# Block fill, row transfers and weight loads in a two-layer trunk on one TensorE-bound core

## The chip, the cores and the metric

The kernel runs on one core of a Trainium2 chip. The metric is the device time of one execution in microseconds (us). Before the change the median of 3 runs is 988.75 us (987.04 to 989.66). Each trace shown is one execution taken by the profiler; line numbers such as L1272 are lines of the kernel before. The engines are PE (TensorE matmul; PEld its weight loads), DVE (VectorE), ACT (ScalarE), POOL (GpSimd) and SP, which here only issues DMAs.

## The reference

Sixteen learned meta tokens are put ahead of 512 tokens of width 1024; two layers follow, and a final RMSNorm. Each layer is `h + branch(rmsnorm(h))`. Layer 0 is gated linear attention with 4 heads (key width 256, value width 512), a decay from a rank-16 gate, and a SiLU gate:

```python
proj = xn @ w_in                               # q, k, v, z, g_lr
lg = log_sigmoid(g_lr @ w_gate_up + b_gate) / 16
# per head, causal:  o_i = sum_{j<=i} (q_i * exp(b_i - b_j)) . k_j  v_j,   b = cumsum(lg)
o = head_rms(o) * gnorm
y = (silu(z) * o) @ w_out
```

Layer 1 is differential softmax attention with 8 heads and a relative-position bias. All is float32.

## The kernel before

**Numbers.** Each float32 operand is split into a high part and a rest (`split`: ACT copies the high part, L270, DVE subtracts, L271), and three matmul passes stand for one product. The input projections use a Strassen-like scheme: a `Unit` handles 256 output columns as seven products of 12 matmuls of 264 columns (`product`, L403). In order they are, for a unit between two others: the one on `s21[0]` (bank bx), on `a12` (by), on `s21[1]` (bv), on `s43[1]` (bx again), the next unit's `a11` (bx), `a22` (by), `s43[0]` (bv). A bank that is written again must first have been read by ACT (`partial`, L424) or DVE (L449, L451, L453).

**Weights.** `load_blocks` (L282 to L288) brings 256 columns of a weight matrix, all 1024 rows, into one of two `raw` buffers, by two DMAs on SP of 512 KB each. The tile is [128, 4, 512]: block 2i+j holds column half i and row half j, and each DMA brings one column half, in pieces of 128 floats. `want_unit` makes from a raw tile, in this order: `a11` (block 0), sums of blocks 2, 3 and 0 (L338), the pair `s21` from the sums, `a12` (block 1), a further sum into block 1 and the pair `s43`, `a22` (block 3). When all of a tile's parts have been written into the program, the next load is, and on the chip it waits for the tile's last reader. `want_plain` takes the two column halves whole; it serves four loads at the start (8 of the 90 DMAs).

**Order of the work.** PE's order is that in which the program is written. `Weaver` holds a queue of background generators (units, output projections). `W.fill(us)` writes background matmuls into the program until their planned time is used up; a step of a unit is three matmuls and counts 0.33, of an output projection six and 0.68. `W.follow((us, fn))` calls a function after so much planned time; a function put on the list `behind` is called right after the next weight load is written, so that its DMA stands behind that load on SP. The order of the other engines is set by a scheduler that goes by priority and readiness.

**The blocks of a head.** `gla_blocks` (L1196 to L1292) goes over 5 token blocks: block 0 has the 16 meta tokens, blocks 1 to 4 have 128 each. `output(b)` does the matmuls (L1208 for block 0; L372 and L1214 otherwise) and the norm: ACT square with sum (L1217), DVE (L513), POOL power (L514), ACT scaled copy (L1219). `rows(b)` transposes the result on PE (L1272), gates it on DVE (L1274) and splits it. Its `fill` pairs are (0.6, 1.2) in heads 1 and 2 (`far`), (1.2, 1.2) in head 3 (`last`) and (1.9, 1.6) in head 0.

```python
for b in range(5):
    W.fill(fill[0] if b else 0.6)
    if prev is not None and (b == 1 or not far):
        rows(b - 1, prev)
    prev = output(b)
    ...
    W.fill(fill[1])
```

**Far rows.** In heads 1 and 2 only block 0 goes through `rows`; blocks 1 and 2, and 3 and 4, are turned by DMA (`far_rows`, L1222). Per block, ACT separates the 16-bit halves (L1233) and issues a write to DRAM (L1234), the pieces. After the second block `W.follow` waits 4.0 us of planned time and puts `turn` on `behind` (L1237). `turn` issues one transposing DMA on SP (L1240) into a part of `b_all` (called keep in the profile), and 11.0 us of planned time later `scaled_rows` gates (L1247) and splits what landed. The output projection that reads the rows is run in the next head; `W.land` forces all that is still open ahead of it.

Of the kernel before, what the change touches and what calls it, by code (L numbers as in the profile page):

```python
# [11 lines left out]
F32 = mybir.dt.float32  # L12
# [8 lines left out]
P = 128  # L21
# [52 lines left out]
class Weaver:  # L74
# [6 lines left out]
    def add(self, gen, us=0.0):  # L81
        self.queue.append(gen)
        self.left += us
        return gen
# [125 lines left out]
def trunk(ctx, tc, x, meta, g_norm, gla_w_in, gla_w_gate_up, gla_b_gate, gla_gnorm, gla_w_out,  # L210
# [3 lines left out]
    act, dve, pe, pool, sp = nc.scalar, nc.vector, nc.tensor, nc.gpsimd, nc.sync  # L214
# [8 lines left out]
    wp = ctx.enter_context(tc.tile_pool(name="wp", bufs=2))  # L223
# [8 lines left out]
    def T(p, shape, dt, tag, **kw):  # L232
        uid[0] += 1
        return p.tile(shape, dt, tag=tag, name=f"{tag}_{uid[0]}", **kw)
# [29 lines left out]
    def split(hi, lo, src, scale=None, keep=False):  # L264

        if keep:
            act.activation(hi, src, AF.Copy)
            kept.append(lambda: dve.tensor_tensor(lo, src, hi.bitcast(F32), op=ALU.subtract))
        elif scale is None:
            act.activation(hi, src, AF.Copy)  # L270
            dve.tensor_tensor(lo, src, hi.bitcast(F32), op=ALU.subtract)  # L271
        else:
            act.activation(hi, src, AF.Copy, scale=scale)
            dve.scalar_tensor_tensor(lo, src, scale, hi.bitcast(F32), op0=ALU.mult, op1=ALU.subtract)
# [4 lines left out]
        sp.dma_start(t, w[r0:r0 + nk * P, c0:c0 + ncol].rearrange("(k p) c -> p k c", p=P))  # L279
        return t  # L280

    def load_blocks(w, c0):  # L282

        t = T(wp, [P, 4, 512], F32, "raw")
        for i in range(2):
            sp.dma_start(t[:, 2 * i:2 * i + 2, :].rearrange("p j (k c) -> p (j k) c", k=4),
                         w[:, c0 + i * P:c0 + (i + 1) * P].rearrange("(k p) c -> p k c", p=P))
        return t  # L288

    W = Weaver()  # L290
    behind = W.behind
# [30 lines left out]

    def block_pair(src, keep=False):
        wh, wl = w_pair([P, 2, 512])
        split(wh, wl, src, keep=keep)
        return [[t[:, i, :] for t in (wh, wl)] for i in range(2)]

    def want_unit(w, c0, calm=False):
        def single(tag, b):
            def fn(raw):  # L330
                t = [T(wp, [P, 512], F32R, tag + part, bufs=1) for part in "hl"]
                with tc.issue_after(W.moved.ins) if calm and b == 0 else ExitStack():
                    split(*t, raw[:, b, :])
                return t
            return Part(tag, fn)

        def add(o, a, b):
            dve.tensor_tensor(o, a, b, op=ALU.add)  # L338

        def sums(raw):  # L340
            t = T(wp, [P, 2, 512], F32, "sum", bufs=1)
            add(t[:, 1, :], raw[:, 2, :], raw[:, 3, :])
            add(t[:, 0, :], t[:, 1, :], raw[:, 0, :])
            add(raw[:, 2, :], raw[:, 2, :], raw[:, 0, :])
            return t

        def outer(raw):
            add(raw[:, 1, :], raw[:, 1, :], su.t[:, 0, :])
            ws.room["sum"] += 1
            return block_pair(raw[:, 1:3, :])  # L350

        a11, a12, a22 = single("a11", 0), single("a12", 1), single("a22", 3)
        su = Part("sum", sums)
        s21 = Part("pair", lambda raw: block_pair(su.t))
        s43 = Part("pair", outer)
        ws.want((w, c0), [a11, su, s21, a12, s43, a22])
        return a11, a12, a22, s21, s43

    def want_plain(w, c0, keep=False):

        def first(raw):
            with behind_gate():
                return block_pair(raw[:, :2, :], keep)

        return ws.want((w, c0), [Part("pair", first),
                                 Part("pair", lambda raw: block_pair(raw[:, 2:, :]))])

    def mm3(ps, a, b, first=True, last=True, **kw):

# [826 lines left out]
    def gla_blocks(hd, s, fill, last, far):  # L1196

        s.y = None

        def val(b):  # L1200
            return [t[:, b - 1, :] for t in s.v]

        @urgent
        def output(b):
            t0, n = BLK[b]
            po = ps_tile()
            if b == 0:
                pe.matmul(po[:NM], s.am, s.vm, start=True, stop=True)  # L1208
            else:
                mm3(po, [t[:, t0 - NM:t0 - NM + P] for t in s.a], val(b), True, False)  # L1210
                for j in range(1, b):
                    c0 = ((b - 1) * (b - 2) // 2 + j - 1) * P
                    mm3(po, [t[:, c0:c0 + P] for t in s.c], val(j), False, False)
                pe.matmul(po, s.cm[:, (b - 1) * P:b * P], s.vm, start=False, stop=True)  # L1214
            on = tmp()[:, :512]
            st = T(tp, [P, 2], F32, "st")
            act.activation(on[:n], po[:n], AF.Square, accum_out=st[:n, 0:1])  # L1217
            rstd_of(st[:n, 1:2], st[:n, 0:1], G_HV, n)
            act.activation(on[:n], po[:n], AF.Copy, scale=st[:n, 1:2])  # L1219
            return on  # L1220

        def far_rows(pair):  # L1222

            yd = T(dp, [2, P, 2, 512], U16, "yd", bufs=2)
            src = yd.rearrange("m p h c -> (m p h) c")
            i = pair[0] - 1
            raw = b_all[:, i:i + 2, :].rearrange("p m c -> p (m c)")[:, :8 * P].rearrange("p (m c) -> p m c", m=4)
            left = [0, 1]

            @urgent  # L1230
            def leave(j, on):
                pl = words(tmp()[:, :512]).rearrange("p (h c) -> p h c", h=2)
                act.activation(pl, words(on).rearrange("p (c h) -> p h c", h=2), AF.Copy)  # L1233
                act.dma_start(yd[j], pl)  # L1234
                left.remove(j)
                if not left:
                    W.follow((4.0, lambda: behind.append((turn, s))), tag=s)  # L1237

            def turn():
                tc.keep_in_program_order(sp.dma_start(words(raw), src, transpose=True))  # L1240
                W.follow((11.0, lambda: scaled_rows(0)), (1.5, lambda: scaled_rows(1)), tag=s)

            def scaled_rows(j):
                t0, n = BLK[pair[j]]
                y = raw[:, :, j * P:(j + 1) * P]
                with tc.issue_after(W.mark.ins):
                    dve.tensor_tensor(y, y, s.z[:, :, t0:t0 + n], op=ALU.mult)  # L1247
                    for m0, m1, hi, lo in s.groups:
                        split(hi[:, :, t0:t0 + n], lo[:, :, t0:t0 + n], y[:, m0:m1, :])

            return leave

        def take_y():

            if not last:
                y = [T(gp, [P, 4, L], F32R, f"y{i}") for i in range(2)]
                return [[t[:, m, :] for m in range(4)] for t in y], [(0, 4, y[0], y[1])]

            qk = [T(gp, [P, 2, L], F32R, tag) for tag in ("qs", "ks")]
            hi = [qk[m // 2][:, m % 2:m % 2 + 1, :] for m in range(4)]  # L1260
            lo = [T(gp, [P, 1, L], F32R, "kd"), T(tp, [P, 1, L], F32R, "t"),
                  T(gp, [P, 1, L], F32R, "vm0"), T(wp, [P, 1, L], F32R, "sum", bufs=1)]
            return [[t[:, 0, :] for t in hi], [t[:, 0, :] for t in lo]], [(m, m + 1, hi[m], lo[m]) for m in range(4)]

        @urgent
        def rows(b, on):
            t0, n = BLK[b]
            if b == 0:
                s.y, s.groups = take_y()
            pt = ps_tile()  # L1270
            for m in range(4):
                pe.transpose(pt[:, m * n:(m + 1) * n], on[:n, m * P:(m + 1) * P], ident[:n, :n])  # L1272
            y = tmp()[:, :512].rearrange("p (m c) -> p m c", m=4)
            dve.tensor_tensor(y[:, :, :n], pt[:, :4 * n].rearrange("p (m c) -> p m c", m=4),  # L1274
                              s.z[:, :, t0:t0 + n], op=ALU.mult)
            for m0, m1, hi, lo in s.groups:
                split(hi[:, :, t0:t0 + n], lo[:, :, t0:t0 + n], y[:, m0:m1, :n])

        prev, leave = None, None
        for b in range(5):  # L1280
            W.fill(fill[0] if b else 0.6)
            if prev is not None and (b == 1 or not far):
                rows(b - 1, prev)
            prev = output(b)
            if far and b:
                if b % 2:
                    leave = far_rows((b, b + 1))
                leave(1 - b % 2, prev)
            W.fill(fill[1])
        if not far:  # L1290
            W.fill(2.0)
            rows(4, prev)  # L1292
# [18 lines left out]
    for hd in range(G_HEADS):  # L1311
        s = heads[hd]
# [610 lines left out]
```

## Time and profile before

| what | value |
|---|---|
| median of 3 runs | 988.75 us (987.04 to 989.66) |
| the profiled execution | 990.28 us, span 988.24 us |
| mean granted clock of TensorE | 0.995 |
| block loads, 512 KB each | 48 of `gla_w_in`, 42 of `diff_w_in` |
| their issue to landing, median | 4.5 and 5.5 us |
| transposes of far rows (L1240) | 4, on SP |
| DMA packets | 159945, of them 145277 under 2 KB |

The page gives busy time per engine over the span. The view of waits lists who stood idle for whom, with total, number and longest. The timeline shows each merged group with start and duration, and in brackets the idle time before it and what ended it. The view of windows gives, for stretches of the span, the length, each engine's busy time with its number of instructions (PE, PEld, DVE, ACT, POOL), the granted clock as a share of full speed, the DMA share and the GB/s. A duration on PE is that of a pipeline: the distance from one start to the next tells what an instruction costs.

### The profile page before, as it was taken

How to read it: one execution, taken by the hardware profiler on the slowest of the kernel's cores; microseconds unless marked ns; L12 is line 12 of the kernel's file. 1: busy time of each engine (PE TensorE's matmuls, PEld its weight loads, DVE VectorE, ACT ScalarE, POOL GpSimd, SP SyncE). 2: the span in 40 equal slices, each digit the busy share in tenths (PEclk: the TensorE clock that was granted, in tenths of full speed). 3: DMA queues.
4: the chain of work that ended last, by engine and by line, in shares of the span. 5: the costliest groups of instructions: out<-in, count | busy, mean ns of one | idle time of the engine just before them, and what ended most of it. 6: DMA issues, size and time to landing. Idle time of an engine off the chain costs nothing. (4 is left out here: it accounts for less than half of the span.)

```text
span 988.2 us, 18164 instructions
## 1 busy us (share of the span) xinstructions
PE 967.4 (98%) x7033; PEld 913.5 (92%) x7033; DVE 776.7 (79%) x1584; ACT 626.6 (63%) x1314; POOL 50.3 (5%) x68
## 2 busy tenths in 40 slices
PE   8999999999999999999999999999999999999997
PEld 8999999989999899999999998898998999988896
DVE  7889985876878599556998885977967879677785
ACT  7776755577636767536657675566764667654583
POOL 1000000000000100000000001001010000000001
PEclk9999999999999999999999999999999999999999
DMA  7332224634473353222332614235253352622212
GB/s 193 87 84 78 58 87 135 134 87 107 129 162 87 94 120 98 75 86 86 97 86 77 153 61 137 80 96 135 87 145 86 97 135 58 174 73 66 86 65 85
DMA packets 159945, 100.45 MB, mean 102 GB/s; under 512 B 41565, under 2 KB 145277, under 8 KB 159856
## 3 DMA queue, kind: packets, MB, share of 16 engines
q1 hardware_dynamic: 155824, 91.71, 34.7%
q10 hardware_dynamic: 4032, 7.55, 2.1%
q8 instruction: 56, 0.92, 0.4%
q14 instruction: 33, 0.27, 0.1%
HBM read 83.64 MB, written 9.67 MB: 94 GB/s over the span
## 5 line engine op out<-in xcount | busy, mean ns | idle before, releaser
L271 DVE TENSOR_TENSOR wl<-raw,wh 128x1024 fp32r<-128x1024 f32 x98 | 119.6, 1222 | 24.6 <-ACT wh L270 17.4
L270 ACT ACTIVATE wh<-raw 128x1024 fp32r<-128x1024 f32 x98 | 103.0, 1054 | 53.3 <-PE by L940 19.1
L403 PE MATMUL bv<-x,wh 128*128 128x264 f32 (+1 forms) x656 | 99.5, 290 | 0.2
L403 PE MATMUL bx<-x,wh 128*128 128x264 f32 (+1 forms) x640 | 95.2, 286 | 1.1 <-ACT wh L270 1.0
L403 PEld LDWEIGHTS bv<-x,wh 128*128 128x128 f32 x656 | 88.2, 192 | 1.3 <-DVE t L449 0.4
L403 PEld LDWEIGHTS bx<-x,wh 128*128 128x128 f32 x640 | 84.9, 189 | 2.4 <-ACT wh L270 1.6
L393 PE MATMUL bx<-x,wh 128*128 128x512 f32 (+1 forms) x256 | 62.5, 386 | 0.0
L271 DVE TENSOR_TENSOR wl<-sum,wh 128x1024 fp32r<-128x1024 f32 x41 | 50.1, 1222 | 14.4 <-ACT wh L270 13.0
L424 ACT ACTIVATE u<-bx 128x264 f32<-128x264 f32 (+1 forms) x120 | 45.3, 379 | 18.5 <-PE bx L403 17.0
L1657 ACT ACTIVATE p<-p,st 128x528 f32<-128x528 f32 (+3 forms) x64 | 36.4, 569 | 32.0 <-DVE st L1655 31.6
L403 PE MATMUL bv<-x,wl 128*128 128x264 f32 (+1 forms) x328 | 55.6, 286 | 0.1
L1693 POOL TENSOR_TENSOR st<-st,mhalf 128x1 f32<-128x1 f32 x32 | 31.1, 973 | 467.4 <-ACT on L1691 389.1
L270 ACT ACTIVATE wh<-sum 128x1024 fp32r<-128x1024 f32 x41 | 43.3, 1056 | 17.1 <-DVE sum L338 9.6
L403 PE MATMUL bx<-x,wl 128*128 128x264 f32 (+1 forms) x320 | 53.9, 285 | 0.0
L393 PEld LDWEIGHTS bx<-x,wh 128*128 128x128 f32 x256 | 44.5, 188 | 8.0
L270 ACT ACTIVATE a11h<-raw 128x512 fp32r<-128x512 f32 x41 | 25.8, 628 | 36.5 <-DMA raw<-in_diff_w_in_dram 18.1
L403 PE MATMUL by<-x,a12h 128*128 128x264 f32 (+1 forms) x320 | 46.7, 286 | 0.5 <-DVE tick L584 0.5
L403 PE MATMUL bx<-x,a11h 128*128 128x264 f32 (+1 forms) x320 | 46.2, 285 | 0.6 <-DVE hT L948 0.6
L403 PEld LDWEIGHTS bv<-x,wl 128*128 128x128 f32 x328 | 46.3, 190 | 0.4 <-issue 0.3
L403 PEld LDWEIGHTS bx<-x,wl 128*128 128x128 f32 x320 | 45.0, 188 | 0.8 <-DVE wl L271 0.5
L403 PEld LDWEIGHTS bx<-x,a11h 128*128 128x128 f32 x320 | 42.0, 188 | 1.4 <-DVE hT L948 0.8
L403 PEld LDWEIGHTS by<-x,a12h 128*128 128x128 f32 x320 | 41.7, 188 | 0.9 <-DVE tick L584 0.9
(483 smaller groups left out, 2640.3 us busy)
## 6 DMA issues: line engine op xcount, KB each, us to landing
raw<-in_gla_w_in_dram SPq DMA_DIRECT2D x48, 512.0 KB, 4.5
raw<-in_diff_w_in_dram SPq DMA_DIRECT2D x42, 512.0 KB, 5.5
raw<-in_diff_w_in_dram SPq DMA_DIRECT2D x11, 1024.0 KB
raw<-in_gla_w_out_dram SPq DMA_DIRECT2D x8, 1024.0 KB, 5.0
raw<-in_diff_w_out_dram SPq DMA_DIRECT2D x8, 1024.0 KB
vd<-planes ACTq DMA_DIRECT2D x12, 268.0 KB, 3.2
vd<-keep ACTq DMA_DIRECT2D x8, 264.0 KB, 2.3
T<-bdr SPq DMA_DIRECT2D x8, 264.0 KB, 5.2
```

The source lines that it names most:

```text
L270: act.activation(hi, src, AF.Copy)
L271: dve.tensor_tensor(lo, src, hi.bitcast(F32), op=ALU.subtract)
L393: pe.matmul(bank, a[:, k, :], b[k] if n0 is None else b[k][:, n0 + i * nn:n0 + (i + 1) * nn], start=n == 0 and ks[0] == 0, stop=n == len(t ...
L403: pe.matmul(bank[:, :x[q].shape[2]], w[p][:, k * P:(k + 1) * P], x[q][:, k, :], start=first and i == 0, stop=i == len(PASSES) - 1, skip_gr ...
L424: W.moved = act.activation(t, self.bx[:, :self.n], AF.Copy, scale=self.sc)
L1657: act.activation(p[:, :nk], p[:, :nk], AF.Exp, scale=-1.0, bias=st[:, m:m + 1], accum_out=st[:, 2 + m:3 + m])
L1693: pool.tensor_tensor(ms, ms, mhalf[:, :1], op=ALU.pow)
```

## The change

Three things are changed. In `gla_blocks`, the fill around block 0 becomes 1.6 behind its output and 1.9 ahead of its rows, in all heads (head 0 had these values). In `far_rows`, `turn` is called itself after the 4.0 us of planned time instead of being put behind the next weight load. `load_blocks` makes its tile [128, 8, 256] and brings a row half in each DMA, in pieces of 256 floats; a block is then a strided view of it (`block`), and the further sum goes into block 0 instead of block 1. The loads of `want_plain` stay by columns (`by_cols`).

```diff
-    def load_blocks(w, c0):
-        t = T(wp, [P, 4, 512], F32, "raw")
-        for i in range(2):
-            sp.dma_start(t[:, 2 * i:2 * i + 2, :].rearrange("p j (k c) -> p (j k) c", k=4),
-                         w[:, c0 + i * P:c0 + (i + 1) * P].rearrange("(k p) c -> p k c", p=P))
+    def load_blocks(w, c0, by_cols=False):
+        t = T(wp, [P, 8, 2 * P], F32, "raw")
...
+        for j in range(2):
+            sp.dma_start(t[:, 4 * j:4 * j + 4, :],
+                         w[512 * j:512 * j + 512, c0:c0 + 2 * P].rearrange("(k p) c -> p k c", p=P))
         return t
+    def block(raw, b):
+        i, j = divmod(b, 2)
+        return raw[:, 4 * j:4 * j + 4, i * P:(i + 1) * P]
...
-            add(t[:, 1, :], raw[:, 2, :], raw[:, 3, :])
+            add(in_rows(t[:, 1, :]), block(raw, 2), block(raw, 3))
...
-            add(raw[:, 1, :], raw[:, 1, :], su.t[:, 0, :])
+            add(block(raw, 0), block(raw, 1), in_rows(su.t[:, 0, :]))
             ws.room["sum"] += 1
-            return block_pair(raw[:, 1:3, :])
+            return block_pair(raw[:, :4, :])
...
                 if not left:
-                    W.follow((4.0, lambda: behind.append((turn, s))), tag=s)
+                    W.follow((4.0, turn), tag=s)
...
-            W.fill(fill[0] if b else 0.6)
+            W.fill(0.6 if b == 0 else 1.9 if b == 1 else fill[0])
...
-            W.fill(fill[1])
+            W.fill(fill[1] if b else 1.6)
```

More of the change, by code (lines that the diff above doesn't have):

```diff
@@ L280, in load_w, with in_rows @@
         return t
-    def load_blocks(w, c0):
-        t = T(wp, [P, 4, 512], F32, "raw")
-        for i in range(2):
-            sp.dma_start(t[:, 2 * i:2 * i + 2, :].rearrange("p j (k c) -> p (j k) c", k=4),
-                         w[:, c0 + i * P:c0 + (i + 1) * P].rearrange("(k p) c -> p k c", p=P))
-        return t
+    def load_blocks(w, c0, by_cols=False):
+        t = T(wp, [P, 8, 2 * P], F32, "raw")
+        if by_cols:
+            t = t.rearrange("p k (i c) -> p (k i) c", c=P)
+            for i in range(2):
+                sp.dma_start(t[:, 8 * i:8 * i + 8, :],
+                             w[:, c0 + i * P:c0 + (i + 1) * P].rearrange("(k p) c -> p k c", p=P))
+            return t
+        for j in range(2):
+            sp.dma_start(t[:, 4 * j:4 * j + 4, :],
+                         w[512 * j:512 * j + 512, c0:c0 + 2 * P].rearrange("(k p) c -> p k c", p=P))
+        return t
+    def block(raw, b):
+        i, j = divmod(b, 2)
+        return raw[:, 4 * j:4 * j + 4, i * P:(i + 1) * P]
+    def in_rows(t):
+        return t.rearrange("p (k c) -> p k c", c=P)
     W = Weaver()
@@ L324, in block_pair @@
         wh, wl = w_pair([P, 2, 512])
-        split(wh, wl, src, keep=keep)
+        if src.shape[1] == 2:
+            split(wh, wl, src, keep=keep)
+        elif src.shape[1] == 8:
+            split(*[t.rearrange("p i (k c) -> p (i k) c", c=P) for t in (wh, wl)], src, keep=keep)
+        else:
+            split(*[t.rearrange("p i (k c) -> p i k c", c=P) for t in (wh, wl)],
+                  src.rearrange("p k (i c) -> p i k c", c=P), keep=keep)
         return [[t[:, i, :] for t in (wh, wl)] for i in range(2)]
@@ L332, in fn @@
                 with tc.issue_after(W.moved.ins) if calm and b == 0 else ExitStack():
-                    split(*t, raw[:, b, :])
+                    split(*[in_rows(o) for o in t], block(raw, b))
                 return t
@@ L341, in sums @@
             t = T(wp, [P, 2, 512], F32, "sum", bufs=1)
-            add(t[:, 1, :], raw[:, 2, :], raw[:, 3, :])
-            add(t[:, 0, :], t[:, 1, :], raw[:, 0, :])
-            add(raw[:, 2, :], raw[:, 2, :], raw[:, 0, :])
+            add(in_rows(t[:, 1, :]), block(raw, 2), block(raw, 3))
+            add(in_rows(t[:, 0, :]), in_rows(t[:, 1, :]), block(raw, 0))
+            add(block(raw, 2), block(raw, 2), block(raw, 0))
             return t
         def outer(raw):
-            add(raw[:, 1, :], raw[:, 1, :], su.t[:, 0, :])
+            add(block(raw, 0), block(raw, 1), in_rows(su.t[:, 0, :]))
             ws.room["sum"] += 1
-            return block_pair(raw[:, 1:3, :])
+            return block_pair(raw[:, :4, :])
         a11, a12, a22 = single("a11", 0), single("a12", 1), single("a22", 3)
@@ L362, in first @@
             with behind_gate():
-                return block_pair(raw[:, :2, :], keep)
-        return ws.want((w, c0), [Part("pair", first),
-                                 Part("pair", lambda raw: block_pair(raw[:, 2:, :]))])
+                return block_pair(raw[:, :8, :], keep)
+        return ws.want((w, c0, True), [Part("pair", first),
+                                       Part("pair", lambda raw: block_pair(raw[:, 8:, :]))])
     def mm3(ps, a, b, first=True, last=True, **kw):
```

## The prediction

> **What bounds the kernel now.** I read the page's totals first, then the waits of PE, then the granted clock.
>
> ```profile
> span 988.2 us, 18164 instructions
> ...
> PE 967.4 (98%) x7033; PEld 913.5 (92%) x7033; DVE 776.7 (79%) x1584; ACT 626.6 (63%) x1314; POOL 50.3 (5%) x68
> ```
>
> TensorE has work in 967.4 of 988.2 us. The matmuls stay, so time can only come out of the 20.8 us in which PE is idle, or out of matmuls that run slower than they could. The waits of PE, longest first:
>
> ```profile
> PE ps L1272 <- ACT t L1219: 3.8, 2, 2.0
> PE ps L372 <- DVE aT L271: 2.0, 2, 1.3
> ...
> PE bx L403 <- ACT wh L270: 1.0, 1, 1.0
> ```
>
> The largest is L1272, the transposes in `rows`: 3.8 us in two waits. The granted clock, in chosen stretches (the columns end with PEclk, DMA share, GB/s):
>
> ```profile
> 105.00:126.00 21.00, 21.00 (x153) 19.65 (x152) 18.21 (x34) 16.22 (x33) 2.02 (x3) 1.00 0.26 68
> ...
> 217.40:220.70 3.30, 3.30 (x16) 3.23 (x15) 1.57 (x6) 2.07 (x5) 0.55 (x1) 0.51 0.64 169
> ...
> 322.99:326.46 3.47, 3.47 (x14) 3.05 (x14) 2.46 (x7) 1.70 (x5) 0.22 (x1) 0.51 0.97 273
> ...
> 981.40:988.20 6.80, 0.00 (x0) 0.00 (x0) 2.06 (x5) 1.68 (x6) 0.55 (x1) 0.78 0.20 77
> ```
>
> The clock is 0.51 in two stretches of some 3.4 us while PE is busy; the drop at the end comes after the last matmul. Now the two waits, on PE, in heads 1 and 2:
>
> ```profile
> 211.36 0.39 PE L1208 MATMUL ps<-vm,am 96*16 96x512 f32 x1
> ...
> 212.34 1.14 PE L403 MATMUL by<-x,a12h 128*128 128x264 f32 x8
> 213.31 0.65 PE L403 MATMUL by<-x,a12l 128*128 128x264 f32 x4
> 215.98 0.41 PE L1272 MATMUL ps<-ident,t 16*128 16x16 f32 x4 [2.02 <-ACT t L1219]
> ...
> 221.08 0.85 PE L372 MATMUL ps<-v,a 128*128 128x512 f32 x3
> ```
>
> ```profile
> 320.35 0.65 PE L403 MATMUL by<-x,a12l 128*128 128x264 f32 x4
> ...
> 322.76 0.42 PE L1272 MATMUL ps<-ident,t 16*128 16x16 f32 x4 [1.76 <-ACT t L1219]
> ...
> 327.85 0.86 PE L372 MATMUL ps<-v,a 128*128 128x512 f32 x3
> ```
>
> Both dips come within 1.5 us after the end of such a wait. Head 0 goes through the same code with more fill, waits for nothing, and keeps 1.00 (105 to 126 us above).
>
> **The change, part by part.**
>
> *The fill.* What the transposes of block 0 wait for, in head 1:
>
> ```profile
> 213.14 0.65 ACT L902 ACTIVATE t<-t 128x528 f32<-128x528 f32 x1 [0.29 <-DVE t L451]
> ...
> 213.69 0.57 ACT L1217 ACTIVATE t<-ps 16x512 f32<-16x512 f32 x1
> ...
> 214.26 0.36 ACT L424 ACTIVATE u<-bx 128x264 f32<-128x264 f32 x1
> ...
> 215.25 0.68 ACT L1219 ACTIVATE t<-ps,st 16x512 f32<-16x512 f32 x1
> ```
>
> From the start of L1208 (211.36) to L1272 (215.98) are 4.62 us, the chain through ACT, DVE, POOL and ACT again. PE's cover is fill in steps of three 264-column matmuls, each step counted as 0.33. Of old, 1.2 gives four steps and 0.6 two: 18 matmuls. The row of four starts at 213.31; at 0.122 us each (the eight before it take 0.97) PE is free at 213.80 and loses 2.18 us. In head 2 it is free at 320.84 and loses 1.92. The change gives 1.6 + 1.9, five and six steps: 33 matmuls, 15 more, 1.83 us. PE then comes to the transposes at 215.63, 0.35 ahead of the data, and in head 2 at 322.67, 0.09 ahead. Saved: 2.18 - 0.35 + 1.92 - 0.09 = **3.66 us**. The 15 matmuls are the unit's next product and the first three of the one after; the bank is free (L451 is done before the second L902 starts), and L424, which reads the bank of the last three, ends at 214.62. They are only moved from the stretch behind the blocks, whose total stays; heads 0 and 3 have no wait there that counts, so I take nothing for them.
>
> *The clock.* From L1272 to the L372 of block 2 lie the transposes, block 1's last four matmuls and 18 of fill: 5.10 us in head 1, 5.09 in head 2. In head 0 the part ahead of the fill takes:
>
> ```profile
> 110.62 0.42 PE L1272 MATMUL ps<-ident,t 16*128 16x16 f32 x4
> ...
> 112.00 0.77 PE L403 MATMUL bv<-x,wh 128*128 128x264 f32 x5
> ```
>
> That is 1.38; with 18 x 0.122 = 2.20 it would be 3.58. Each dip costs 1.5 us, together **3.03**. The stretches with the other waits of the list, of 1.0 and of 1.3 us, have none:
>
> ```profile
> 235.00:318.00 83.00, 80.95 (x662) 79.98 (x661) 67.16 (x126) 47.95 (x82) 0.00 (x0) 1.00 0.55 134
> ...
> 848.00:914.00 66.00, 64.16 (x384) 55.96 (x383) 46.80 (x101) 35.53 (x88) 4.29 (x6) 1.00 0.36 98
> ```
>
> So a dip needs a wait between 1.3 and 1.8 us, and what stays is 0.35 and 0.09: I expect both to go.
>
> A rule speaks against this term. The Trainium skill ("TensorE: Matmul & The Clock Gate", section "HAM oscillation — how this bites in real kernels") puts the gap that throttles at over some 3.4 us, and the same page lets its window run freely. By that rule waits of 2.02 and 1.76 us would not throttle, the dips would have another cause, and only 3.66 us would be saved. The trace disagrees: 0.51 right behind both gaps, and no other dip before the last matmul.
>
> *The row transfers.* `turn` used to be put behind the next weight load, and now goes to SP itself, 4.0 us of planned PE time after the second piece. Rows of before:
>
> ```profile
> 235.57 0.99 SPq L286 DMA_DIRECT2D raw<-in_gla_w_in_dram  x2
> ...
> 236.67 6.78 SPq L1240 DMA_TRANSPOSE keep<-yd  x1
> ...
> 248.11 0.38 SPq L279 DMA_DIRECT2D raw<-in_gla_w_out_dram  x1
> ...
> 248.59 4.54 SPq L1240 DMA_TRANSPOSE keep<-yd  x1
> ...
> 249.99 0.67 DVE L1247 TENSOR_TENSOR keep<-keep,z 128x512 f32<-128x512 f32 x1
> ...
> 250.69 0.63 ACT L270 ACTIVATE y<-keep 128x512 fp32r<-128x512 f32 x1
> ...
> 261.28 1.25 PE L403 MATMUL bx<-x,wh 128*128 128x264 f32 x8 [0.99 <-ACT wh L270]
> ```
>
> ```profile
> yd<-t ACTq DMA_DIRECT2D x8, 256.0 KB, 2.0
> ...
> keep<-yd SPq DMA_TRANSPOSE x4, 8.7
> ```
>
> Counted in steps from the output of block 0: the load is issued at step 26 in both versions, since it hangs on a product's end. The outputs of blocks 2 and 4 move from steps 12 and 24 to 17 and 29. The first turn comes due 13 steps after block 2's output: old at 25, ahead of the load, new at 30, behind it. Deferred as of old it would now wait for the load at 248.11. Sent directly it is behind the same load as before. The second comes due at step 42, some 235.5 us with the waits gone, and goes when SP has issued the first (about 237): some 8 us sooner against its surroundings. Queued behind it on SP is the load of 248.11, which waits for its buffer until about 244.7 in new time; the turn's issue (4.5 to 6.8 us) ends ahead of that, so nothing is delayed. The added wait is that for the pieces, which land 2.0 us after leaving, within the 4.0. DVE takes the rows 34 steps later (12.4 us), landing takes 8.7. Sum: 0. Bounds: better than nothing by the 1.0 at 261.28; worse by the rival below.
>
> *The loads.* 82 of the 90 block loads get 512 pieces of 1 KB instead of 1024 of 512 B; their operands become runs of 128 at a stride of 256.
>
> ```profile
> 299.00:303.50 4.50, 4.50 (x39) 4.50 (x39) 4.15 (x7) 3.38 (x7) 0.00 (x0) 1.00 0.89 237
> ...
> 436.00:440.50 4.50, 4.50 (x39) 4.48 (x38) 2.48 (x6) 2.00 (x3) 0.00 (x0) 1.00 0.76 226
> ```
>
> A pair of 512 B loads (299 us) and one 1 KB load of the same size (436 us) both need about 4.5 us, so I take no gain, within 0.5 us each way. It could count only where a load is waited for and PE feels it:
>
> ```profile
> 906.56 0.69 DVE L338 TENSOR_TENSOR sum<-raw 128x512 f32<-128x512 f32 x1 [4.73 <-DMA raw<-in_diff_w_in_dram]
> ...
> 910.45 0.73 PE L372 MATMUL ps<-v,aT 128*128 128x256 f32 x4 [1.31 <-DVE aT L271]
> ```
>
> So between 0.5 gained and 0.5 lost there; I take 0. For the stride, the same shape with and without it:
>
> ```profile
> L338 DVE TENSOR_TENSOR raw<-raw x41: 671/684/690, 64.4 to 924.7; 128x512 f32<-128x512 f32 x41
> ```
>
> ```profile
> L1247 DVE TENSOR_TENSOR keep<-keep,z x8: 672/679/686, 250.0 to 377.7; 128x512 f32<-128x512 f32 x8
> ```
>
> L1247 works in place on such runs: 679 ns against 684; on ACT the y<-keep above, strided on both sides, takes 0.63. The stride is free.
>
> **Sum.** 3.66 + 3.03 = 6.7 us. The profiled execution took 990.28 us, 2.04 around its span of 988.24, so span 981.5 and 983.6 in all. It lay 1.5 above the median of 988.75; the same saving from that gives **982.1 us**.
>
> **The rivals.**
> - *The dips stay* (their cause is the small transposes, or the window falls otherwise): 988.75 - 3.66 = 985.1. For it: head 0 shows only one case without a dip. Against it: head 0 has the same transposes. Chance 0.10.
> - *Other waits go too*: half of those at 261 and 910 us and 0.35 + 0.09 more: 982.1 - 1.6 = 980.5, up to 3 us below the forecast. Chance 0.10.
> - *The fill does little*: the extra steps bring a split (1.06 us of ACT) ahead of L1219, and more than a microsecond of each wait is left; with the dips gone in one head only, about 987. Chance 0.09.
> - *Slower*: the second turn does fall behind a load that waits for its buffer. Issued at 245 instead of 237 it lands at 253.7, while DVE, which works in order, has come to the rows by 248; DVE stands 5.6 us. If that passes whole to PE, with a dip of 1.5, two heads lose 14.2: 988.75 - 6.7 + 14.2 = 996.3. It decides once the issue starts after about 239.3 (248 less 8.7). Against it: SP is idle in that stretch now. Chance 0.06.
>
> **How the numbers follow.** Forecast 0.65, rivals 0.10, 0.10, 0.09, 0.06. A change under 0.3% (985.8 to 991.7) can't be told from none. Faster: forecast, second rival and 0.06 of the first = 0.81; same: the rest of the first and the third = 0.13; slower: 0.06. The range: down to 979.5 by the second rival with both of its waits, up to 986.5 by the first with the loads' 0.5 and a new wait of the size of that at 261 us.
>
> **What would show it.** Right: L1272 gone from PE's waits or under 0.4 each; clock 1.00 from 205 to 330 us; the second L1240 about 6 us after the first; L338 and L271 on raw still 0.68; loads to landing within 0.5 of before. Wrong: a new PE wait over 1.5 us with a dip behind it, or L1247 waiting for its transfer.

## The result, and the profile after

The changed kernel takes 985.55 us (median of 6 runs, 984.69 to 987.41) against 989.14 us (6 runs, 987.04 to 989.79). The ratio is 0.9968, with a 95% interval of 0.9955 to 0.9981: 3.6 us by the medians where 6.7 were forecast. The time lies within the stated range, but the saving is only about half of the forecast one. The profiled execution took 985.99 us, its span 984.2.

In the changed file the lines behind the new helpers are 19 higher: the transposes of `rows` are L1291, unit products L422, the gating of far rows L1266, the transposes of `to_tokens` L853 and L854. The totals of the page, and the longest waits of PE:

```profile
span 984.2 us, 18134 instructions
...
PE 966.5 (98%) x7033; PEld 914.1 (93%) x7033; DVE 776.8 (79%) x1584; ACT 625.7 (64%) x1314; POOL 50.5 (5%) x68
```

```profile
PE ps L854 <- DVE c L271: 2.3, 1, 2.3
PE bx L422 <- ACT wh L270: 2.3, 1, 2.3
...
PE ps L391 <- DVE aT L271: 0.6, 1, 0.6
```

L1291 is gone from the list: PE no longer waits for the transposes of block 0. Two waits of 2.3 us stand in its place, one in the stage of scores of head 2, one in that of head 3. The granted clock in four stretches (the third value from the right, ahead of the DMA share and the GB/s):

```profile
208.00:235.00 27.00, 27.00 (x191) 25.24 (x191) 18.97 (x37) 21.96 (x41) 2.74 (x5) 1.00 0.34 107
314.00:342.00 28.00, 28.00 (x199) 26.24 (x199) 18.62 (x37) 23.57 (x43) 2.74 (x5) 1.00 0.45 132
...
259.00:264.00 5.00, 4.81 (x27) 4.81 (x28) 2.99 (x4) 1.56 (x4) 0.00 (x0) 0.66 0.43 147
364.00:370.00 6.00, 5.48 (x32) 5.21 (x33) 4.89 (x11) 2.31 (x5) 0.00 (x0) 0.72 0.57 178
```

In the blocks of heads 1 and 2 PE now has no gap and the full clock. Behind the two new waits the clock dips, as it did behind the old ones. SP shows what moved:

```profile
230.52 11.24 SPq L1259 DMA_TRANSPOSE keep<-yd  x2
...
243.96 0.38 SPq L279 DMA_DIRECT2D raw<-in_gla_w_out_dram  x1
```

Both turns now go one after the other ahead of the load of the output weights; before, the second came behind it at 248.59. No load is held up, as forecast (243.96 here, 244.06 with deferred turns and the rest of the change). But the 11.24 us hold a wait: the last pieces left at 234.92, and SP stood until they had landed, so the second turn started at 239.88 and not at about 237.

```profile
SPq L1259 <- DMA yd<-t: 6.7, 2, 4.2
```

```profile
239.88 1.87 SPq L1259 DMA_TRANSPOSE keep<-yd  x1
```

What comes sooner with the second turn is its rows. The new wait of head 2, on DVE, ACT and PE:

```profile
250.86 0.70 DVE L1266 TENSOR_TENSOR keep<-keep,z 128x512 f32<-128x512 f32 x1
...
253.05 0.68 DVE L271 TENSOR_TENSOR y<-keep,y 128x512 fp32r<-128x512 f32 x1
...
254.39 0.69 DVE L271 TENSOR_TENSOR y<-keep,y 128x512 fp32r<-128x512 f32 x1
...
255.00 0.69 DVE L1266 TENSOR_TENSOR keep<-keep,z 128x512 f32<-128x512 f32 x1
...
255.60 0.69 DVE L357 TENSOR_TENSOR raw<-raw,sum 128x512 f32<-128x512 f32 x1
...
257.40 0.63 ACT L270 ACTIVATE y<-keep 128x512 fp32r<-128x512 f32 x1
...
258.09 1.99 ACT L270 ACTIVATE wh<-raw 128x1024 fp32r<-128x1024 f32 x2
...
259.19 1.85 PE L422 MATMUL bx<-x,wh 128*128 128x264 f32 x8 [2.25 <-ACT wh L270]
```

PE waits for the split of a weight pair (wh). ACT makes it after a y<-keep, the split of a far row, and it needs the sum raw<-raw,sum. On DVE that sum stands behind the gating of blocks 3 and 4 (250.86 and 255.00) and the splits of blocks 2 and 3 (253.05 and 254.39). Before the change the same sum and split came with the rows of blocks 3 and 4 still ahead, and a wait of 0.99 us followed:

```profile
258.02 0.69 DVE L338 TENSOR_TENSOR raw<-raw,sum 128x512 f32<-128x512 f32 x1
...
260.17 1.06 ACT L270 ACTIVATE wh<-raw 128x1024 fp32r<-128x1024 f32 x1
...
265.65 0.68 DVE L1247 TENSOR_TENSOR keep<-keep,z 128x512 f32<-128x512 f32 x1
...
267.64 0.69 DVE L1247 TENSOR_TENSOR keep<-keep,z 128x512 f32<-128x512 f32 x1
```

### The profile page after: what moved, and what is told of

Same layout as the page of the kernel before. It is cut to its first block, busy times and chain, and to the rows that moved or that the text cites. A ratio compares the mean times of both kernels' runs of the same rounds, so it can differ in the third digit from the quotient of the medians.

```text
span 984.2 us, 18134 instructions
## 1 busy us (share of the span) xinstructions
PE 966.5 (98%) x7033; PEld 914.1 (93%) x7033; DVE 776.8 (79%) x1584; ACT 625.7 (64%) x1314; POOL 50.5 (5%) x68
## 2 busy tenths in 40 slices
DMA packets 117961, 100.45 MB, mean 102 GB/s; under 512 B 41565, under 2 KB 103293, under 8 KB 117872
## 5 line engine op out<-in xcount | busy, mean ns | idle before, releaser
L422 PE MATMUL bv<-x,wh 128*128 128x264 f32 (+1 forms) x656 | 97.9, 287 | 0.6 <-DVE z L470 0.6
L422 PE MATMUL bx<-x,wh 128*128 128x264 f32 (+1 forms) x640 | 95.8, 287 | 2.7 <-ACT wh L270 2.3
L422 PEld LDWEIGHTS bx<-x,wh 128*128 128x128 f32 x640 | 85.0, 189 | 4.2 <-ACT wh L270 2.8
L422 PEld LDWEIGHTS bv<-x,wh 128*128 128x128 f32 x656 | 86.5, 189 | 1.2 <-DVE z L470 0.9
L422 PE MATMUL bv<-x,wl 128*128 128x264 f32 (+1 forms) x328 | 55.4, 285 | 0.2 <-PEq L1321 0.2
L422 PE MATMUL bx<-x,wl 128*128 128x264 f32 (+1 forms) x320 | 54.3, 286 | 0.0
L422 PE MATMUL by<-x,a12h 128*128 128x264 f32 (+1 forms) x320 | 46.5, 285 | 0.0
L422 PEld LDWEIGHTS bv<-x,wl 128*128 128x128 f32 x328 | 46.1, 189 | 0.4 <-issue 0.3
L422 PEld LDWEIGHTS bx<-x,wl 128*128 128x128 f32 x320 | 45.5, 189 | 0.8 <-DVE wl L271 0.5
L422 PE MATMUL bx<-x,a11h 128*128 128x264 f32 (+1 forms) x320 | 46.1, 285 | 0.0
L422 PEld LDWEIGHTS bx<-x,a11h 128*128 128x128 f32 x320 | 42.1, 188 | 0.6
L422 PEld LDWEIGHTS by<-x,a12h 128*128 128x128 f32 x320 | 41.7, 188 | 0.0
```

The source lines that it names most:

```text
L422: pe.matmul(bank[:, :x[q].shape[2]], w[p][:, k * P:(k + 1) * P], x[q][:, k, :], start=first and i == 0, stop=i == len(PASSES) - 1, skip_gr ...
```

## The experiments

Theory A: the second turn, sent sooner, brings the rows of blocks 3 and 4 into a stretch where DVE and ACT are needed for weight splits and scores, and that makes the two new waits. Theory B: they come from the new layout of the raw blocks. Theory C: they come from the 15 matmuls moved forward. All times are medians, beside runs of the kernel before on the same chip (989.29 us, 15 runs, for the first four; 988.90, 23 runs, for the last four).

**The fill alone.** The turns stay deferred; since the outputs come later in planned time, they are put behind after 2.6 us, which leaves each behind the same load as before (this goes for the next run too).

```diff
-            W.fill(fill[0] if b else 0.6)
+            W.fill(0.6 if b == 0 else 1.9 if b == 1 else fill[0])
...
-            W.fill(fill[1])
+            W.fill(fill[1] if b else 1.6)
...
-                    W.follow((4.0, lambda: behind.append((turn, s))), tag=s)
+                    W.follow((2.6, lambda: behind.append((turn, s))), tag=s)
```

> The kernel before with the new fill about block 0, the turns still behind the weight loads (2.6 us of planned time instead of 4.0 ahead of the deferral, so that each stands behind the same load as before). Theory A (the new 2.3 us waits of the changed kernel come from the second turn and its rows being moved forward): both old L1272 waits and both dips go, no new wait above 1.2 us appears, 6.7 us saved, about 982.4 us, ratio 0.993. Theory B (they come from the new layout of the raw blocks): the same 982.4. Theory C (they come from the 15 matmuls moved forward): a wait of about 2.2 us in the stage of scores of heads 2 and 3 with a dip each, about 985.5, ratio 0.9965.

Measured: 984.26 us (983.47 to 984.83), ratio 0.9956 (0.9943 to 0.9970). L1272 (0.2 us are left) and its dips are gone, and no 2.3 us wait appears, so C falls. But 5.0 us are saved, not 6.7. The wait at L372 is longer than before and has a dip of its own, and the one at L835 is new. The waits, and the clock behind the first of them:

```profile
PE ps L372 <- DVE aT L271: 1.7, 1, 1.7
...
PE ps L835 <- DVE c L271: 1.2, 1, 1.2
```

```profile
906.00:908.00 2.00, 2.00 (x11) 2.00 (x10) 2.00 (x5) 1.01 (x5) 0.79 (x1) 0.50 0.00 0
```

The L372 wait, 1.65 us, ended at 904.24; it was 1.31 before, with no dip.

**Fill and loads,** the changed kernel with only the turns as before.

```diff
-                    W.follow((4.0, turn), tag=s)
+                    W.follow((2.6, lambda: behind.append((turn, s))), tag=s)
```

> The changed kernel with the turns put behind the weight loads again (after 2.6 us of planned time). Theory A: the two new waits of 2.3 us and their dips are gone, about 982 us, ratio 0.993. Theory B: both stay, about 985.5, ratio 0.9965. Theory C: both stay, about 985.5.

Measured: 982.08 us (981.15 to 983.29), ratio 0.9935 (0.9922 to 0.9949), the forecast time of the whole change, but by chance: the fill gives less than forecast, and the loads make up for it. The 2.3 us waits are gone: head 2 has none, and head 3 keeps half of its wait:

```profile
360.12 0.27 PE L854 MATMUL ps<-ident,t 128*32 128x128 f32 x1 [1.11 <-DVE c L271]
```

B falls with it, since the layout is the new one here. Sending the turns directly costs the changed kernel 985.55 - 982.08 = 3.5 us.

**Fill and turns,** the changed kernel with `load_blocks` and its users as before.

> The changed kernel with the loads by columns again: new fill and turns sent directly. Theory A: both new waits of about 2.3 us with a dip each, about 985.8, ratio 0.9968. Theory B: neither, about 982.4, ratio 0.993. Theory C: both, 985.8.

Measured: 988.08 us (986.05 to 988.75), ratio 0.9986 (0.9977 to 0.9995). The two waits are there (2.26 us at 259.15, and 2.3 at L835), as A and C had it. It is 2.3 us slower than expected: the loads by rows, which I had at nothing, are missing here.

**The loads alone,** the kernel before with `load_blocks` and its users changed.

> The kernel before with the loads by rows alone. Theory A: both old waits at L1272 (2.0 and 1.8 us) and their dips stay, nothing new, between 0 and 1.5 us saved where DVE waited for a load at 906 us, about 988.3, ratio 0.999. Theory B: the two new 2.3 us waits stand beside the old ones, about 993, ratio 1.004. Theory C: as A.

Measured: 984.80 us (984.23 to 985.27), ratio 0.9963 (0.9950 to 0.9977). This edit alone saves at least as much as the whole change, and no theory had that. Its waits at the transposes of block 0 are 1.28 and 1.31 us instead of 2.02 and 1.76, and no dip follows:

```profile
210.00:235.00 25.00, 23.72 (x164) 21.91 (x163) 16.50 (x34) 20.33 (x36) 3.12 (x5) 1.00 0.23 75
314.00:342.00 28.00, 26.69 (x190) 24.94 (x189) 17.80 (x35) 23.25 (x42) 3.13 (x5) 1.00 0.40 121
```

The reason stands further up the same chain. First the kernel before, then this one, from DVE's wait for a load to the transposes:

```profile
209.32 0.69 DVE L338 TENSOR_TENSOR sum<-raw 128x512 f32<-128x512 f32 x1 [1.46 <-DMA raw<-in_gla_w_in_dram]
...
211.74 0.43 DVE L449 SCALAR_TENSOR_TENSOR t<-by,u 128x264 f32<-128x264 f32 x1
```

```profile
208.72 0.69 DVE L357 TENSOR_TENSOR sum<-raw 128x512 f32<-128x512 f32 x1 [0.98 <-DMA raw<-in_gla_w_in_dram]
...
211.14 0.43 DVE L468 SCALAR_TENSOR_TENSOR t<-by,u 128x264 f32<-128x264 f32 x1
...
211.75 0.63 ACT L921 ACTIVATE t<-t 128x528 f32<-128x528 f32 x1
...
213.10 0.57 ACT L1236 ACTIVATE t<-ps 16x512 f32<-16x512 f32 x1
...
215.68 0.42 PE L1291 MATMUL ps<-ident,t 16*128 16x16 f32 x4 [1.28 <-ACT t L1238]
```

While DVE waits for the load, the addition that the gate needs (L449, here L468) stands behind it in DVE's order, although its operands are there: in the kernel before, PE's product in by ends at 209.34 and ACT's u at 208.59, and L449 starts at 211.74. On ACT the norm stands behind the gate. The load was issued at 203.19 in one trace and 203.35 in the other: 6.13 us to the sum, and 5.37. In the other traces the same load takes 5.91 to 6.31 us with pieces of 512 B and 5.18 to 5.34 with pieces of 1 KB.

**The layout alone,** pieces of 512 B into the new tile:

```diff
-        for j in range(2):
-            sp.dma_start(t[:, 4 * j:4 * j + 4, :],
-                         w[512 * j:512 * j + 512, c0:c0 + 2 * P].rearrange("(k p) c -> p k c", p=P))
+        for i in range(2):
+            sp.dma_start(t[:, :, i * P:(i + 1) * P],
+                         w[:, c0 + i * P:c0 + (i + 1) * P].rearrange("(k p) c -> p k c", p=P))
```

> The kernel before with the new raw tile and the new operands, but each DMA bringing a column half in pieces of 512 B as before. Theory P (the loads' gain comes from pieces that land some 0.7 us sooner, so that DVE, the gate and the norm ahead of the transposes of block 0 are sooner): loads land as before (4.5 and 5.5 us), the two waits stay near 2.0 and 1.8 us with a dip each, about 989, ratio 1.000. Theory L (it comes from the layout: the further sum into block 0 and another order on DVE): waits of 1.3 us, no dip, 984.8, ratio 0.996.

Measured: 992.26 us (988.21 to 994.13), ratio 1.0034 (1.0021 to 1.0047). P holds: the gain goes with the way the weights are loaded and not with the layout. (Which half a DMA brings, rows or columns, changes together with the size of the pieces; no run separates the two.) The sum starts 6.31 us after the load's issue (203.80), and the waits are longer than before:

```profile
210.11 0.69 DVE L357 TENSOR_TENSOR sum<-raw 128x512 f32<-128x512 f32 x1 [2.37 <-DMA raw<-in_gla_w_in_dram]
```

```profile
PE ps L1291 <- ACT t L1238: 4.4, 2, 2.3
```

The layout by itself costs 3.4 us here; the operands take 0.68 to 0.69 us as before. In this stretch the load leaves 0.6 us later, and on DVE a further sum (213.81) now stands ahead of a split and of the step of the norm, which starts 0.41 us behind its input instead of 0.10. What makes the rest of the 3.4 us is not shown. Median landing is 4.5 and 5.5 us in the kernel before, 4.2 and 5.5 here, and with 1 KB pieces in the run with the loads alone:

```profile
raw<-in_gla_w_in_dram SPq DMA_DIRECT2D x48, 512.0 KB, 4.1
raw<-in_diff_w_in_dram SPq DMA_DIRECT2D x42, 512.0 KB, 4.7
```

With the new fill the medians are 4.4 and 5.5 us for 512 B, 4.7 and 4.8 for 1 KB. So the medians show a gain for `diff_w_in` alone; for `gla_w_in` the evidence is the single load above.

**Half of the fill,** 6 matmuls more instead of 15. All turns by DMA are put on `behind` after 3.3 us, those of `turn_by_dma` (L565) included; they stand behind the same loads as before:

```diff
-                W.follow((4.0, lambda: behind.append((turn, None))))
+                W.follow((3.3, lambda: behind.append((turn, None))))
...
-            W.fill(fill[0] if b else 0.6)
+            W.fill(0.6 if b == 0 else 1.2 if b == 1 else fill[0])
...
-                    W.follow((4.0, lambda: behind.append((turn, s))), tag=s)
+                    W.follow((3.3, lambda: behind.append((turn, s))), tag=s)
```

> The kernel before with 1.2 instead of 0.6 us of fill ahead of the rows of block 0 in heads 1 and 2: 6 matmuls more, 0.73 us (turns deferred after 3.3 us of planned time, behind the same loads as before). The waits become about 1.3 and 1.0 us. Theory D (a dip follows only a wait longer than some 1.3 to 1.7 us): no dips, 1.5 + 3.0 us saved, about 984.6, ratio 0.9955. Theory E (the dips have another cause in this place, such as the small transposes): both dips stay, only 1.5 us saved, about 987.6, ratio 0.9985.

Measured: 989.44 us (987.54 to 991.31), ratio 1.0012 (1.0001 to 1.0023): neither time. On the dips D holds: waits of 1.09 and 0.81 us, and a clock of 1.00 behind both. Much of the time is taken back in head 3, by an L835 wait that had been absent before, with a dip; on DVE a weight split (wl) stands ahead of the operands:

```profile
363.65 1.22 DVE L271 TENSOR_TENSOR wl<-raw,wh 128x1024 fp32r<-128x1024 f32 x1
...
364.90 0.28 DVE L382 TENSOR_TENSOR cm<-ps,cm 32x128 fp32r<-32x128 f32 x1
...
365.56 0.28 DVE L271 TENSOR_TENSOR c<-ps,c 128x128 fp32r<-128x128 f32 x1
...
365.99 0.37 PE L835 MATMUL ps<-ident,t 128*32 128x128 f32 x1 [2.58 <-DVE c L271]
```

```profile
210.00:235.00 25.00, 23.91 (x166) 22.11 (x165) 16.12 (x31) 18.61 (x34) 3.27 (x5) 1.00 0.28 81
314.00:342.00 28.00, 27.19 (x193) 25.39 (x192) 17.58 (x35) 21.93 (x40) 3.27 (x5) 1.00 0.40 109
364.00:370.00 6.00, 4.01 (x23) 4.04 (x23) 5.66 (x12) 2.98 (x6) 0.00 (x0) 0.72 0.63 174
```

Here the rows of blocks 3 and 4 of head 2 come only at 372.91, so a wait of this kind in head 3 doesn't need them: it comes where the weight split falls just ahead of these operands, as it does in the changed kernel too (wl at 362.77, c at 363.92). With deferred turns and the new fill and loads, that split is done at 356.35. Why this edit puts it there I have not found out.

**The turns alone,** `W.follow((4.0, turn), tag=s)` in the kernel before.

> The kernel before with the turns sent directly, and nothing else. Theory A: the old waits at the transposes of block 0 with their dips stay, and the two new waits of about 2.3 us in the stage of scores of heads 2 and 3 come with a dip each: about 4 to 6 us more, 993 to 995, ratio 1.004 to 1.006. If the new waits need the fill or the loads as well: 989, ratio 1.000.

Measured: 994.57 us (993.53 to 996.44), ratio 1.0068 (1.0054 to 1.0083), as A had it. Beside L1272 (1.72 and 1.76 us) stand, in heads 2 and 3:

```profile
261.97 1.23 PE L403 MATMUL bx<-x,wh 128*128 128x264 f32 x8 [2.45 <-ACT wh L270]
```

```profile
370.17 0.27 PE L835 MATMUL ps<-ident,t 128*32 128x128 f32 x1 [1.69 <-DVE c L271]
373.01 2.93 PE L1178 MATMUL ps<-qs,kd 128*128 128x128 f32 x12 [1.48 <-DVE v L271]
```

**Late rows,** the changed kernel, both turns sent directly, but the rows of blocks 3 and 4 taken later:

```diff
-                W.follow((11.0, lambda: scaled_rows(0)), (1.5, lambda: scaled_rows(1)), tag=s)
+                W.follow((11.0 if pair[0] == 1 else 17.0, lambda: scaled_rows(0)), (1.5, lambda: scaled_rows(1)), tag=s)
```

> The changed kernel, turns sent directly as there, but the rows of blocks 3 and 4 gated and split 17.0 instead of 11.0 us of planned time after their turn, about where they stood before the change. Theory A1 (the two 2.3 us waits come from the rows' DVE and ACT work standing ahead of the scores' and splits' in their in-order queues): the waits fall to about 1.1 us as in the run with deferred turns, no dip, about 982 us, ratio 0.993. Theory A2 (they come from the earlier transfers themselves): waits and dips stay, about 985.5, ratio 0.9965.

Measured: 982.08 us (981.49 to 982.57), ratio 0.9938 (0.9926 to 0.9951). The transfers run as early as in the changed kernel (both from 230.33 us), and the time is that of the run with deferred turns. The rows of blocks 3 and 4 come behind the sum, which DVE now starts at 250.99 instead of 255.60, and head 3 keeps half of its wait:

```profile
250.99 0.69 DVE L357 TENSOR_TENSOR raw<-raw,sum 128x512 f32<-128x512 f32 x1
...
256.28 0.69 DVE L1266 TENSOR_TENSOR keep<-keep,z 128x512 f32<-128x512 f32 x1
```

```profile
PE ps L854 <- DVE c L271: 1.1, 1, 1.1
```

So A1 is shown: it is the place of the rows' work on DVE and ACT, not the transfers. This version and fill with loads beat both kernels.

## Why only half of the forecast saving came

**The fill: right.** With the fill alone 0.2 us of the waits at the transposes of block 0 are left, where 0.35 and 0.09 had been forecast. In the changed kernel none is left; the loads land sooner there.

**The clock: mechanism right, size too large.** Removing or only shortening the waits removes the dips. But 3.03 us holds for an execution with both dips, and the profiled one was such. Over 38 runs of the kernel before, the 14 with a mean clock of 0.995 or less take 989.8 us on average, and the 10 with 0.998 or more take 987.6: 2.2 us between them. If the latter have no dips, the median contained only part of what I subtracted; only one run was traced, so this is argued from the mean clock. With the gaps of 1.65 and 1.2 us 5.0 are left of the 6.7 us that I put on the fill; no run splits the missing 1.7. The shortest wait with a dip behind it is 1.65 us; the longest without one is 1.36, at L1700 (684.52) in the run with half of the fill. (In the run with the turns alone the waits of 1.69 and 1.48 us in head 3 share one dip.) The Trainium skill ("TensorE: Matmul & The Clock Gate", section "HAM oscillation — how this bites in real kernels") has the gap that throttles at over some 3.4 us; these traces disagree. The same page of the Trainium skill ("Part 1: The HAM clock gate") says that the window runs freely, and that the point at which the clock rises after a start therefore varies from run to run. Here mean clocks from 0.994 to 0.999 for one kernel show that the clock varies between runs too; that the window is the reason no run shows.

**The row transfers: this step failed.** "Sum: 0." I followed the transfers on SP, and there the forecast held: the same load ahead of the first turn, the second right behind it, nothing delayed. (The pieces did not land within the 4.0 us: the last took 4.9, and the second turn started at 239.88 instead of about 237, without holding up a load.) I then only asked whether the rows' data would be there in time. The question not asked was what the rows themselves do when they come sooner: in each of two heads four operations on DVE and two on ACT, most of which come to stand ahead of a weight split that PE needs. Even the place was in my list, as a wait of 0.99 us at 261.28; I had it as a thing that might get better. It went from 0.99 to 2.25 us, past the length from which a dip follows, and with head 3 the step costs 3.5 us. The rival with a slower end named a late transfer as its mechanism, and this isn't what happened. The sign that I had named for being wrong, a new PE wait over 1.5 us with a dip behind it, is what came.

**The loads: sized wrongly as well.** "I take no gain." The load ahead of the transposes of block 0 takes 5.18 to 5.37 us to its sum with pieces of 1 KB and 5.91 to 6.31 with 512 B. I compared an old pair with one DMA of 1 MB by their transfer time, about 4.5 us both, and looked for a wait for a load only where PE stood soon after (906 us). The wait of 1.46 us that DVE had for a load at 209.32 was the first link of the very chain that I quoted from its middle. Alone the edit saves 4.5 us, on top of the fill 2.2. The Trainium skill ("DMA: Bandwidth & Descriptors", section "Specifications") puts the least size for line rate at 512 B. Taken as the size that suffices, it would leave nothing to gain above 512 B; these runs show a gain of 0.5 to 1.1 us for that load.

So the parts are: fill -5.0, loads on top of it -2.2, turns on top of both +3.5, in sum -3.7 against -3.6 measured. That the time fell into the range is luck: the loads gave more than the fill lacked, and the turns took 3.5 us back. The parts don't add up as single edits (-5.0, -4.5, +5.7), because fill and loads both shorten the same waits, and a dip can go only once.

## What to carry to other kernels

When a step is moved earlier, list the instructions that follow from it on each in-order engine, and look at what they will stand ahead of; that its own data are ready is only half of the question. Follow the chain behind a PE wait up to its first link, across engines: here ACT's lateness was DVE's, and DVE's was a load's. A gap on PE of 1.65 us or more cost more than its length here, so it pays to shorten it below the length that brings a dip, even where it can't be closed.

## What the runs showed of the hardware

Waits of 1.09, 1.28, 1.31 and 1.36 us left the granted clock at 1.00, while waits of 1.65 to 2.6 us were followed by a clock of 0.5 for some 3.4 us in the traced executions; the mean clock of other runs suggests that it isn't so in each. Loads of 512 KB of `diff_w_in` in pieces of 1 KB landed in 4.7 and 4.8 us (medians of two runs) where pieces of 512 B took 5.5, with 117961 instead of 159945 packets in the execution. The issue of a row turn kept SP for 1.87 us in one case and 6.78 in another.
